# One layer of a hybrid streaming encoder: the low halves of every second piece of MLP weights come from an adding DMA

## The chip, the cores and the metric

The kernel runs on one core of a Trainium2 chip. The metric is the device time of one execution, in microseconds (us). Before the change the median of three runs is 1284.4 us (1284.13 to 1284.76).

## The reference

One layer with 256 tokens and 2048 model columns. A token mixer (a gated delta rule on eight heads, and an HGRN2 recurrence on eight heads) stands between two residual additions, and an MLP follows. The part that the change touches is the MLP:

```
def squared_relu_mlp(n, w1, w2):
    return jnp.square(jax.nn.relu(n @ w1)) @ w2

        n = rms_norm(h, norm_ffn_w[layer])
        h = h + squared_relu_mlp(n, w_ff1[layer], w_ff2[layer])
    return rms_norm(h, norm_final_w)
```

`w_ff1` is 2048 x 8192 and `w_ff2` is 8192 x 2048, both float32: 64 MB each, read once.

## The kernel before, in words

**Two halves of every weight.** TensorE multiplies in a rounded float32 format (fp32r). To keep float32 accuracy each operand is split in two: `hi` is the operand rounded to fp32r, and `lo` is what the rounding lost, `lo = w - hi`. A product is then made of three parts: hi times hi, hi times lo and lo times hi. For weights, `split` (L109 to L123) makes the two halves: ACT copies `w` into `hi` with the cast (L117), DVE subtracts `hi` from `w` into `lo` (L118).

**Stages.** Input projection and token mixer take up to about 460 us, the output projection up to 564 us, the first MLP product (FF1, `w_ff1`) from 564 to 927 us, the second (FF2, `w_ff2`) from 927 us to the end.

**Pieces.** The MLP weights come in 128 tiles `w` of 128 x 2048 (1 MB), 64 for each product, loaded by SP's DMA queue into a ring of three buffers. Each tile is split in two pieces of 128 x 1024. `hi` and `lo` of a piece live in two rings of three buffers each (`spool`). A piece of FF1 gives TensorE 8 matmuls with `hi` as the stationary operand (L700, 512 columns of `hT`, which holds the hi and lo of the activations side by side) and 8 with `lo` (L701, 256 columns), into four PSUM banks that belong to four blocks of FF columns; eight pieces make a group (`fg`), and groups take turns with two sets of four banks. A piece of FF2 gives 12 matmuls of 512 columns (L717): 8 with `hi`, 4 with `lo`, each with a block of the split activation `gs` as the stationary operand. The last three of FF2's 64 tiles are held and multiplied at the end (`held`); two of them, the tiles 61 and 62 counted from 0, are split into a buffer of their own (`keep`).

**What sets the order.** The kernel is written with a tile framework that puts the instructions of each engine in an order at build time. It goes by a timeline of its own, and it also gives each tile one of the buffers of its ring by that timeline. Waits between engines follow from reads and writes: whoever writes into a buffer again waits for the last reader of what it held. Each engine executes its own list in order. SP's list in the MLP is the loads of `w` alone; a load waits until the splits of the tile that held the buffer, three tiles earlier, are done. POOL has no work in the MLP until the last normalization.

Of the kernel before, what the change touches and what calls it, by code (L numbers as in the profile page):

```python
# [8 lines left out]
F32R = mybir.dt.float32r  # L9
AF = mybir.ActivationFunctionType  # L10
ALU = mybir.AluOpType
# [4 lines left out]
P = 128  # L16
# [57 lines left out]
def hybrid_block(ctx: ExitStack, tc: tile.TileContext, x, xt, w_in, w_ab, params, w_out, w_ff1, w_ff2,  # L74
                 norm_final_w, consts, out):
    nc = tc.nc
    PE, ACT, DVE, POOL, SP = nc.tensor, nc.scalar, nc.vector, nc.gpsimd, nc.sync
# [8 lines left out]
    spool = ctx.enter_context(tc.tile_pool(name="spool", bufs=3))  # L86
# [12 lines left out]
    def wtile():  # L99
        return wpool.tile([P, 2048], F32, tag="w", name="w")  # L100

    def acc_a():
        return psA.tile([P, 512], F32, tag="acc", name="acc")
# [7 lines left out]
    def split(w, n, hi=None, lo=None, pieces=1, eng=DVE):  # L111

        if hi is None:
            hi = spool.tile([P, n], F32R, tag="hi", name="hi")
            lo = spool.tile([P, n], F32R, tag="lo", name="lo")
        if pieces == 1:
            ACT.copy(hi, w)  # L117
            eng.tensor_tensor(out=lo, in0=w, in1=hi.bitcast(F32), op=ALU.subtract)  # L118
        else:
            for i in range(pieces):  # L120
                s = slice(i * n // pieces, (i + 1) * n // pieces)
                split(w[:, s], None, hi[:, s], lo[:, s], eng=eng)
        return hi, lo  # L123


# [85 lines left out]
    def gates():  # L211
        ab = spool.tile([P, KT, 2, 16], F32R, tag="hi", name="ab")
        split(wab, None, ab[:, :, 0, :], ab[:, :, 1, :])
        pab = mx("pab")
        for k in range(KT):
# [49 lines left out]
    def project(base, hd, chunk, dsts):  # L265
        accs = [acc_a() for _ in range(2)]
        for kh in range(2):
            first = base == 0 and hd == 0 and chunk == 0
            if first:
                w = w_first[kh]  # L270
            else:
                w = wtile()
                SP.dma_start(w, w_in[((base > 0) * NH + hd) * 4 + chunk * 2 + kh])
            for q in range(2):
                hi, lo = split(w[:, q * 1024:(q + 1) * 1024], 1024, pieces=2 if first else 1, eng=POOL if first else DVE)
                hi = hi.rearrange("p (k g c) -> p k g c", k=4, g=2)
                lo = lo.rearrange("p (k g c) -> p k g c", k=4, g=2)
                for kk in range(4):
                    k = kh * 8 + q * 4 + kk
                    for g in range(2):  # L280
                        PE.matmul(accs[g], lhsT=hi[:, kk, g, :], rhs=xT[:, k, :], start=(k == 0), stop=False)  # L281
                        PE.matmul(accs[g][:, T:], lhsT=lo[:, kk, g, :], rhs=xT[:, k, 0:T],  # L282
                                  start=False, stop=(k == KT - 1))
        if first:
            row_scales()
        for g in range(2):
            lot = mp.tile([P, T], F32, tag="lot", name="lot", bufs=2)
            ACT.copy(lot, accs[g][:, T:])
            DVE.tensor_tensor(out=lot, in0=accs[g][:, 0:T], in1=lot, op=ALU.add)
            (POOL if base == 0 else DVE).tensor_tensor(out=dsts[g], in0=lot, in1=rB, op=ALU.mult)  # L290
# [341 lines left out]
    def acc_b():  # L632
        return psB.tile([P, 512], F32, tag="accb", name="accb")
# [9 lines left out]
    for nh in range(2):  # L643
        accs = [acc_a() for _ in range(4)]
        for kp in range(8):
            w = wtile()
            SP.dma_start(w, w_out[nh * 8 + kp])
            for kk in range(2):
                k = 2 * kp + kk
                hi, lo = split(w[:, kk * 1024:(kk + 1) * 1024], 1024)  # L650
# [34 lines left out]
    def g(f):  # L685
        return gt[f // NG][:, f % NG, :]

    nfw = fp.tile([P, D], F32, tag="nfw", name="nfw")
    for fg in range(NF // 4):
        accs = [acc_a() if fg % 2 == 0 else acc_b() for _ in range(4)]  # L690
        for kq in range(4):
            w = wtile()
            SP.dma_start(w, w_ff1[fg * 4 + kq])
            for q in range(2):
                hi, lo = split(w[:, q * 1024:(q + 1) * 1024], 1024)
                for kk in range(2):
                    k = 4 * kq + 2 * q + kk
                    for f in range(4):
                        cs = slice(kk * 512 + f * P, kk * 512 + (f + 1) * P)
                        PE.matmul(accs[f], lhsT=hi[:, cs], rhs=hT[:, k, :], start=(k == 0), stop=False)  # L700
                        PE.matmul(accs[f][:, T:], lhsT=lo[:, cs], rhs=hT[:, k, 0:T], start=False, stop=(k == KT - 1))  # L701
        for f in range(4):
            lot = fp.tile([P, T], F32, tag="lotf", name="lotf", bufs=2)
            ACT.copy(lot, accs[f][:, T:])
            DVE.tensor_tensor(out=lot, in0=accs[f][:, 0:T], in1=lot, op=ALU.add)
            DVE.scalar_tensor_tensor(out=g(4 * fg + f), in0=lot, scalar=0.0, in1=lot, op0=ALU.max, op1=ALU.mult)
# [6 lines left out]
    def ff2(f, hf, c, gs, hl):  # L713
        hi, lo = hl[c // 2]
        cs = slice((c % 2) * 512, (c % 2 + 1) * 512)
        for a, ww in ((0, hi), (T, hi), (0, lo)):
            PE.matmul(accs[hf][c], lhsT=gs[:, a + hf * P:a + hf * P + P], rhs=ww[:, cs],  # L717
                      start=(f == 0 and a == 0 and ww is hi), stop=(f == NF - 1 and ww is lo))

    keep = None  # L720
    for f in range(NF):
        w = wtile()
        SP.dma_start(w, w_ff2[f])
        gs = fp.tile([P, 2 * T], F32R, tag="gs", name="gs", bufs=4)
        split(g(f), None, gs[:, 0:T], gs[:, T:])
        n = f - (NF - TAIL)
        if n == 0:
            keep = fp.tile([P, TAIL - 1, 2, D], F32R, tag="g0", name="keep")
        hl = []
        for q in range(2):  # L730
            qs = slice(q * 1024, (q + 1) * 1024)
            if 0 <= n < TAIL - 1:
                hl.append(split(w[:, qs], None, keep[:, n, 0, qs], keep[:, n, 1, qs]))
            else:
                hl.append(split(w[:, qs], 1024))
        if n >= 0:
            held.append((f, gs, hl))
            continue
        for q in range(2):
            for hf in range(2):  # L740
                for c in (2 * q, 2 * q + 1):
                    ff2(f, hf, c, gs, hl)
# [4 lines left out]
    for hf in range(2):  # L747
        pieces = [(c * 512, (c + 1) * 512) for c in range(3)]
# [74 lines left out]
```

## Time and profile before

| | |
|---|---|
| median of 3 runs | 1284.4 us (1284.13 to 1284.76) |
| the profiled execution, its own time | 1285.84 us |
| its span in the trace | 1283.9 us |
| mean granted TensorE clock in it | 0.992 |
| TensorE (PE) busy | 1252.5 us (98%) |
| DVE, ACT, POOL busy | 858.5 (67%), 673.8 (52%), 180.4 us (14%) |
| DMA | 229.65 MB, mean 179 GB/s |

How to read it: PE is matmuls, PEld the loading of their stationary operands, SPq and POOLq the instructions with which SP and POOL start DMAs. Each row of a group names the line of the kernel, the engine, the operation, what it writes and reads, and how often. "Idle before" is the time in which that engine had nothing to do just ahead of such an instruction, with the instruction that ended the wait. A DMA's "landing" is counted from its issue to the arrival of its last byte's signal.

### The profile page before, as it was taken

To read this page: it belongs to the slowest core of one execution; us is meant where nothing else is said; L and a number is where in the kernel's file an instruction comes from. 1 tells how busy PE (TensorE), PEld (TensorE's weight loads), DVE (VectorE), ACT (ScalarE), POOL (GpSimd) and SP (SyncE) were. 2 spreads that over 40 slices of the span, in tenths; PEclk is the share of its full clock that TensorE was granted. 3 is DMA by queue.
4 is the path that set the end of the run, shared out by engine and by line. 5 is a ranking of instruction groups with operands and counts; after the bars stand their busy time and mean duration, and the time that the engine had idled before them with its cause. 6 is when DMAs were issued, how large, how long until landed. Compare 5 with 4: busy or idle time off the path is not lost.

```text
span 1283.9 us, 18498 instructions
## 1 busy us (share of the span) xinstructions
PE 1252.5 (98%) x7290; PEld 1063.2 (83%) x7290; DVE 858.5 (67%) x1200; ACT 673.8 (52%) x972; POOL 180.4 (14%) x224
## 2 busy tenths in 40 slices
PE   6999999998899999999999999999999999999997
PEld 5888888877788887888888888888888888888885
DVE  8789999888867996565556555565555555555556
ACT  7567677655556874454444443444444444444453
POOL 4233433278301121000000000000000000000000
PEclk9999999998999999999999999999999999999999
DMA  7455555543423644455555555555555555555552
GB/s 289 166 160 184 174 180 192 171 140 131 149 100 131 217 151 168 154 203 191 194 173 190 196 174 189 197 175 186 197 195 190 188 191 192 194 194 197 197 200 95
DMA packets 34646, 229.65 MB, mean 179 GB/s; under 512 B 4408, under 2 KB 5184, under 8 KB 7808
## 3 DMA queue, kind: packets, MB, share of 16 engines
q1 hardware_dynamic: 32256, 225.32, 49.8%
q0 software_dynamic: 1728, 2.11, 1.3%
q8 instruction: 57, 0.93, 0.3%
q10 hardware_dynamic: 576, 1.05, 0.2%
q14 instruction: 29, 0.24, 0.1%
HBM read 225.83 MB, written 2.63 MB: 178 GB/s over the span
## 4 chain that ended last, share of the span: by engine, by line
PE 91%; DVE 3%; POOL 3%; issue 2%; DMA 1%; ACT 0%; SPq 0%; POOLq 0%; DVEq 0%; ACTq 0%
PE acc L281 15%; PE acc L717 14%; PE accb L717 13%; PE accb L700 9%; PE acc L700 9%; PE acc L282 8%; PE acc L655 7%; PE accb L701 5%; PE acc L701 5%; POOL Xt L419 1%; POOL X L421 1%; PE pd L575 1%; DVE xT L163 1%; DMA big<-in_xt_dram 1%; PE pk L363 1%
## 5 line engine op out<-in xcount | busy, mean ns | idle before, releaser
L118 DVE TENSOR_TENSOR lo<-w,hi 128x1024 fp32r<-128x1024 f32 x408 | 511.5, 1255 | 364.6 <-ACT hi L117 364.1
L117 ACT CAST hi<-w 128x1024 fp32r<-128x1024 f32 (+1 forms) x416 | 432.6, 1042 | 447.3 <-PE accb L717 177.2
L281 PE MATMUL acc<-xT,hi 128*128 128x512 f32 x1024 | 363.2, 401 | 9.6 <-ACT hi L117 8.5
L282 PE MATMUL acc<-xT,lo 128*128 128x256 f32 x1024 | 282.8, 285 | 4.8 <-DVE lo L118 4.7
L281 PEld LDWEIGHTS acc<-xT,hi 128*128 128x128 f32 x1024 | 191.0, 190 | 49.1 <-ACT hi L117 8.5
L282 PEld LDWEIGHTS acc<-xT,lo 128*128 128x128 f32 x1024 | 194.8, 191 | 12.1 <-DVE lo L118 6.2
L700 PE MATMUL acc<-hT,hi 128*128 128x512 f32 x512 | 181.3, 399 | 0.0
L700 PE MATMUL accb<-hT,hi 128*128 128x512 f32 x512 | 180.8, 398 | 0.0
L717 PE MATMUL accb<-hi,gs 128*128 128x512 f32 x496 | 170.6, 389 | 0.0
L701 PE MATMUL accb<-hT,lo 128*128 128x256 f32 x512 | 143.2, 281 | 0.0
L701 PE MATMUL acc<-hT,lo 128*128 128x256 f32 x512 | 142.8, 281 | 0.0
L717 PE MATMUL acc<-hi,gs 128*128 128x512 f32 x496 | 133.4, 389 | 0.0
L700 PEld LDWEIGHTS accb<-hT,hi 128*128 128x128 f32 x512 | 96.1, 188 | 23.9
L700 PEld LDWEIGHTS acc<-hT,hi 128*128 128x128 f32 x512 | 96.1, 188 | 23.4
L159 POOL TENSOR_TENSOR fin<-fin,cst 128x1 f32<-128x1 f32 x2 | 1.1, 566 | 777.0 <-PE accb L717 769.5
L717 PEld LDWEIGHTS acc<-hi,gs 128*128 128x128 f32 x496 | 93.0, 188 | 19.4
L717 PEld LDWEIGHTS accb<-hi,gs 128*128 128x128 f32 x496 | 93.1, 188 | 19.3
L701 PEld LDWEIGHTS acc<-hT,lo 128*128 128x128 f32 x512 | 96.5, 189 | 0.2
L701 PEld LDWEIGHTS accb<-hT,lo 128*128 128x128 f32 x512 | 96.6, 189 | 0.1
L717 PE MATMUL accb<-lo,gs 128*128 128x512 f32 x248 | 95.8, 389 | 0.0
L717 PE MATMUL acc<-lo,gs 128*128 128x512 f32 x248 | 77.2, 389 | 0.0
L717 PEld LDWEIGHTS acc<-lo,gs 128*128 128x128 f32 x248 | 46.6, 188 | 9.7
(248 smaller groups left out, 1323.6 us busy)
## 6 DMA issues: line engine op xcount, KB each, us to landing
w<-in_w_ff_dram SPq DMA_DIRECT2D x128, 1024.0 KB, 4.9
w<-in_w_in_dram SPq DMA_DIRECT2D x62, 1024.0 KB, 5.0
w<-in_w_out_dram SPq DMA_DIRECT2D x16, 1024.0 KB, 4.9
big<-in_xt_dram SPq DMA_DIRECT2D x4, 512.0 KB, 7.9
w<-in_w_in_dram SPq DMA_DIRECT2D x4, 512.0 KB, 8.1
h<-in_x_dram SPq DMA_DIRECT2D x2, 1024.0 KB, 9.2
dt<-scr_g POOLq DMA_DIRECT2D x8, 128.0 KB, 5.6
nfw<-in_norm_final_w_dram SPq DMA_DIRECT2D x1, 1024.0 KB, 4.7
```

The lines of the kernel that those rows point to most:

```text
L117: ACT.copy(hi, w)
L118: eng.tensor_tensor(out=lo, in0=w, in1=hi.bitcast(F32), op=ALU.subtract)
L163: DVE.scalar_tensor_tensor(out=dst[:, k, T:2 * T], in0=pt, scalar=wcol, in1=dst[:, k, 0:T].bitcast(F32), op0=ALU.mult, op1=ALU.subtract)
L281: PE.matmul(accs[g], lhsT=hi[:, kk, g, :], rhs=xT[:, k, :], start=(k == 0), stop=False)
L282: PE.matmul(accs[g][:, T:], lhsT=lo[:, kk, g, :], rhs=xT[:, k, 0:T], start=False, stop=(k == KT - 1))
L363: PE.matmul(pk0, lhsT=R[:, 1, 0:P], rhs=qk.rearrange("p a t -> p (a t)"), start=True, stop=True)
L419: POOL.tensor_tensor(out=t3, in0=X[:, j, j + 1:].unsqueeze(2).to_broadcast([np_, nr, ncol]), in1=X[:, j, 0:ncol].unsqueeze(1).to_broadcast ...
L421: POOL.tensor_tensor(out=X[:, j + 1:, 0:ncol], in0=X[:, j + 1:, 0:ncol], in1=t3, op=ALU.subtract)
L655: PE.matmul(accs[2 * hf + c], lhsT=st, rhs=ww[:, c * 512:(c + 1) * 512], start=(k == 0 and a == 0 and ww is hi), stop=(k == 2 * NH - 1 and ...
L700: PE.matmul(accs[f], lhsT=hi[:, cs], rhs=hT[:, k, :], start=(k == 0), stop=False)
L701: PE.matmul(accs[f][:, T:], lhsT=lo[:, cs], rhs=hT[:, k, 0:T], start=False, stop=(k == KT - 1))
L717: PE.matmul(accs[hf][c], lhsT=gs[:, a + hf * P:a + hf * P + P], rhs=ww[:, cs], start=(f == 0 and a == 0 and ww is hi), stop=(f == NF - 1 a ...
```

## The change

`split_ff` takes the place of `split` for the pieces of both MLP products (not for the two `keep` tiles). It counts pieces. An odd one (the first, third and so on, which is the first half of its tile `w`) is split as before. For an even one (the second half of its tile)

- ACT writes `-w`, cast to fp32r, into `lo` (`AF.Copy` with a scale of -1),
- POOL starts a DMA that reads the same 128 x 1024 weights from DRAM again and adds them onto `lo`, so that it holds `w - hi`,
- ACT copies `w` into `hi`.

DVE has no part in an even piece. There are 252 pieces that `split_ff` sees, so 126 such DMAs, 64 in FF1 and 62 in FF2, of 512 KB each.

```
+    pieces = [0]
+
+    def split_ff(w, src):
+
+        pieces[0] += 1
+        if pieces[0] % 2:
+            return split(w, 1024)
+        hi = spool.tile([P, 1024], F32R, tag="hi", name="hi")
+        lo = spool.tile([P, 1024], F32R, tag="lo", name="lo")
+        ACT.activation(lo, w, AF.Copy, scale=-1.0)
+        POOL.dma_start(lo, src, accum_op=ALU.add)
+        ACT.copy(hi, w)
         return hi, lo
...
             w = wtile()
             SP.dma_start(w, w_ff1[fg * 4 + kq])
             for q in range(2):
-                hi, lo = split(w[:, q * 1024:(q + 1) * 1024], 1024)
+                qs = slice(q * 1024, (q + 1) * 1024)
+                hi, lo = split_ff(w[:, qs], w_ff1[fg * 4 + kq, :, qs])
...
             if 0 <= n < TAIL - 1:
                 hl.append(split(w[:, qs], None, keep[:, n, 0, qs], keep[:, n, 1, qs]))
             else:
-                hl.append(split(w[:, qs], 1024))
+                hl.append(split_ff(w[:, qs], w_ff2[f, :, qs]))
```

In the changed kernel the lines of the diff stand 14 to 15 lines lower: L700 and L701 become L715 and L716, L717 becomes L732; the negated copy is L134, the DMA L135, the copy into `hi` L136. In what follows pieces are counted from 0 over both products, so the even pieces are those of DVE and the odd ones those of the DMA.

The build orders the engines anew. Three places are shown. In the rows the number behind a name is that of the tile, and a row ends with the semaphores that its instruction waits for: DMASW is a DMA issued by POOL, DMAHW one issued by SP.

**PE in FF1**, at the start of a second half of a tile `w`, before:

```order
L700 MATMUL accb_6595<-hT_4998,hi_6705 128x512 [waits Activation_49]
L701 MATMUL accb_6595<-hT_4998,lo_6706 128x256 [waits DVE_49]
L700 MATMUL accb_6596<-hT_4998,hi_6705 128x512
L701 MATMUL accb_6596<-hT_4998,lo_6706 128x256
L700 MATMUL accb_6597<-hT_4998,hi_6705 128x512
L701 MATMUL accb_6597<-hT_4998,lo_6706 128x256
```

and at the same piece now:

```order
L715 MATMUL accb_6615<-hT_4998,hi_6727 128x512 [waits Activation_49]
L715 MATMUL accb_6616<-hT_4998,hi_6727 128x512
L715 MATMUL accb_6617<-hT_4998,hi_6727 128x512
L715 MATMUL accb_6618<-hT_4998,hi_6727 128x512
L716 MATMUL accb_6615<-hT_4998,lo_6728 128x256 [waits DMASW5_49]
L716 MATMUL accb_6616<-hT_4998,lo_6728 128x256
```

Four matmuls with `hi` come first, then four with `lo`, of which the first waits for the DMA, then the rest in turns. This holds for two of the four odd pieces of a group of eight. The other two, and one even piece, are mixed. Counted from piece 26 on, PE takes in order: 26; 27 (hi x4, wait, rest); 28; 29 (hi x4, wait, rest); 30; 31 (hi x4 only); 32; 33 (hi x4 only); 31 (wait, the remaining 12); 33 (wait, the remaining 12); and then 34, which stands to its group as 26 does.

**ACT in FF1**, the casts of four consecutive pieces before:

```order
L117 CAST hi_6685<-w_6683 128x1024 [waits DMAHW2_49,PE_49,Activation_49]
L117 CAST hi_6705<-w_6683 128x1024 [waits DVE_49,PE_49]
L117 CAST hi_6727<-w_6725 128x1024 [waits DMAHW3_49,DVE_49,PE_49]
L117 CAST hi_6747<-w_6725 128x1024 [waits DVE_49,PE_49]
L117 CAST hi_6789<-w_6787 128x1024 [waits DMAHW4_49,DVE_49,PE_49]
```

and now:

```order
L117 CAST hi_6707<-w_6705 128x1024 [waits DMAHW2_49,PE_49,Activation_49]
L136 CAST hi_6727<-w_6705 128x1024 [waits PE_49,Activation_49]
L134 ACTIVATE lo_6728<-w_6705 128x1024 [waits DMASW1_49,PE_49]
L117 CAST hi_6750<-w_6748 128x1024 [waits DMAHW3_49,PE_49,Activation_49]
L136 CAST hi_6770<-w_6748 128x1024 [waits DVE_49,PE_49]
L134 ACTIVATE lo_6771<-w_6748 128x1024 [waits DMASW3_49,PE_49]
```

The negated copy stands behind the copy into `hi` of the same piece, although the source has it first. What it waits for on PE is the last matmul with the `lo` that its buffer held: for piece 29 that of piece 26, for 31 that of 28, for 33 that of 30, and for 35 (which stands to its group as 27 does) that of 31. The copy into `hi` ahead of it waits for the last matmul with `hi` of the same earlier piece, which is the instruction just before. The POOL DMA follows the negated copy at once; and the load of the tile `w` three tiles on, in SP's list, waits for the same negated copy, since that is the last reader of its buffer.

**PE in FF2**, most of a piece, before:

```order
L717 MATMUL acc<-hi,gs 128x512 [waits Activation_49]
L717 MATMUL acc<-hi,gs 128x512 x3
L717 MATMUL accb<-hi,gs 128x512
L717 MATMUL acc<-lo,gs 128x512 [waits DVE_49]
L717 MATMUL acc<-lo,gs 128x512
L717 MATMUL accb<-hi,gs 128x512
L717 MATMUL accb<-lo,gs 128x512
```

and now, with the parts of four pieces in turn:

```order
L732 MATMUL acc<-hi,gs 128x512 [waits Activation_49]
L732 MATMUL acc<-hi,gs 128x512 x3
L732 MATMUL accb<-hi,gs 128x512 x4
L732 MATMUL acc<-lo,gs 128x512 [waits DMASW4_49]
L732 MATMUL acc<-lo,gs 128x512
L732 MATMUL accb<-lo,gs 128x512 x2
L732 MATMUL acc<-hi,gs 128x512 x4
L732 MATMUL accb<-hi,gs 128x512 x4
L732 MATMUL acc<-lo,gs 128x512 [waits DVE_49]
L732 MATMUL acc<-lo,gs 128x512
L732 MATMUL accb<-lo,gs 128x512 x2
```

These 24 matmuls repeat through FF2: 8 with the `hi` of an even piece, 4 with the `lo` of an earlier odd piece (this is the wait for the DMA), 8 with the `hi` of the next odd piece, 4 with the `lo` of the even piece that the 24 began with. The odd pieces use two of the three `lo` buffers in turn and the even ones the third. So a negated copy waits for the last `lo` matmul of the odd piece before the last one, and the matmuls that need its DMA come 44 matmuls later. On ACT it stands behind the cast of an even piece that can be made 4 matmuls earlier.

More of the change, by code (lines that the diff above doesn't have):

```diff
@@ L122, in split @@
                 split(w[:, s], None, hi[:, s], lo[:, s], eng=eng)
+        return hi, lo
+    pieces = [0]
[8 more added lines that the diff above has]
+        ACT.copy(hi, w)
         return hi, lo
```

## The prediction

> **What bounds the kernel now.** I read the table of busy time by stage first, over the two MLP products (columns: length; busy time with instructions for PE, PEld, DVE, ACT, POOL; granted clock; DMA share; GB/s):
>
> ```profile
> 564.00:926.00 362.00, 362.00 (x2059) 314.09 (x2058) 204.22 (x268) 159.47 (x205) 0.00 (x0) 1.00 0.54 189
> 927.00:1250.00 323.00, 323.00 (x1426) 267.45 (x1425) 168.34 (x185) 145.65 (x182) 0.00 (x0) 1.00 0.55 194
> ```
>
> PE is busy in all of both stretches at a clock of 1.00. DVE and ACT are about half idle, POOL does nothing, the DMA engines are busy a little over half. The groups of the first stretch say what the splits cost and what they wait for:
>
> ```profile
> L118 DVE TENSOR_TENSOR lo<-w,hi 128x1024 fp32r<-128x1024 f32 x128 | 156.7, 1225 | 156.0 <-ACT hi L117 156.0
> L117 ACT CAST hi<-w 128x1024 fp32r<-128x1024 f32 x128 | 134.3, 1050 | 188.7 <-PE accb L700 95.0 <-PE acc L700 92.0 <-PE acc L655 1.7
> ```
>
> DVE waits for ACT, ACT waits for PE to give a buffer back: the splits run ahead of PE until the ring is full. So the DVE work that is taken away is off the path, and its removal alone is worth nothing here. What counts is whether the new way delivers `lo` in time.
>
> PE's own rate comes from its timeline. FF1, one piece:
>
> ```profile
> 649.74 0.40 PE L700 MATMUL accb<-hT,hi 128*128 128x512 f32 x1
> ...
> 652.23 0.40 PE L700 MATMUL accb<-hT,hi 128*128 128x512 f32 x1
> ...
> 652.46 0.28 PE L701 MATMUL accb<-hT,lo 128*128 128x256 f32 x1
> ...
> 652.57 0.40 PE L700 MATMUL accb<-hT,hi 128*128 128x512 f32 x1
> ...
> 652.66 1.05 ACT L117 CAST hi<-w 128x1024 fp32r<-128x1024 f32 x1 [1.78 <-PE accb L700]
> ```
>
> From 649.74 to 652.57 are eight pairs: 2.83 us a piece, 0.235 for a `hi` matmul and 0.118 for a `lo`. ACT starts its cast 0.20 us after PE's next matmul began (652.66 against 652.46): that is the price of handing a buffer back. FF2, three pieces of 12 matmuls:
>
> ```profile
> 1000.21 1.07 PE L717 MATMUL acc<-hi,gs 128*128 128x512 f32 x4
> ...
> 1002.93 1.07 PE L717 MATMUL acc<-hi,gs 128*128 128x512 f32 x4
> ...
> 1005.65 1.07 PE L717 MATMUL acc<-hi,gs 128*128 128x512 f32 x4
> ```
>
> 2.72 us a piece, 0.227 a matmul.
>
> **The change part by part.** *PE's new order* costs nothing by itself. Four `lo` matmuls in a row occur before in pairs:
>
> ```profile
> 15.29 0.63 PE L281 MATMUL acc<-xT,hi 128*128 128x512 f32 x2
> 15.76 0.40 PE L282 MATMUL acc<-xT,lo 128*128 128x256 f32 x2
> 15.99 0.40 PE L281 MATMUL acc<-xT,hi 128*128 128x512 f32 x1
> ```
>
> Two and two take 0.70 us, as two pairs in turns do.
>
> *ACT* gets 126 negated copies. Nearest rows: the cast above, 1.05 us, and an ACTIVATE of this size, 1.048:
>
> ```profile
> L172 ACT ACTIVATE junk<-big x4: 1039/1048/1063, 6.9 to 22.0; 128x1024 f32<-128x1024 f32 x4
> ```
>
> 126 x 1.05 = 132 us, on an engine that is idle for 202 of the first 362 us and 177 of the next 323: covered as work. As latency it counts, below. *DVE* loses 126 x 1.225 = 154 us that nobody waited for: 0.
>
> *Room.* How long may a negated copy, its DMA and the signal take, from the matmul that frees the `lo` buffer to the matmul that needs the new content? From PE's order in FF1 (a piece 2.83, four `hi` 0.94, the remaining twelve 1.88):
> - piece 27 (or 35: the remainder of 33, the whole of 34, four `hi`): 1.88 + 2.83 + 0.94 = 5.65
> - piece 29: two pieces and four `hi`: 6.60
> - piece 31: three pieces and twice four `hi`: 10.37
> - piece 33: four `hi`, a piece, four `hi`, a remainder: 6.59
> - FF2: 44 x 0.227 = 9.99
>
> *What has to fit in it.* In FF1 0.20 for the release, 1.05 for the copy into `hi` that stands ahead in ACT's list and is released only one matmul earlier, 1.05 for the negated copy, 0.10 for the two hand-overs to POOL and to PE (an estimate: half of the 0.20 just seen), and the DMA's landing D: 2.40 + D. In FF2 the cast ahead is already done: 1.35 + D.
>
> *D.* No DMA of before adds, and none of this size goes through POOL. The rows near it, first POOL's 256 KB load on an otherwise quiet stretch, in its timeline and in the DMA table of the window 253 to 262 us:
>
> ```profile
> 256.02 0.59 POOL L410 DMA_DIRECT2D X<-scr_a  x1
> ...
> 259.54 1.63 POOL L413 TENSOR_SCALAR_AFFINE_SELECT X<-X 64x1024 f32<-64x1024 f32 x1 [2.26 <-DMA X<-scr_a]
> ```
> ```profile
> q0 software_dynamic: 80, 0.26, 9.9%
> X<-scr_a POOLq DMA_DIRECT2D x1, 256.0 KB, 3.5
> ```
>
> It lands in 3.5 us, of which its packets take 9.9% of 9 us = 0.89: 2.6 us are fixed, the issue included. Then the weight loads, in the DMA table of FF1:
>
> ```profile
> q1 hardware_dynamic: 9354, 68.11, 53.5%
> w<-in_w_ff_dram SPq DMA_DIRECT2D x63, 1024.0 KB, 4.9
> ```
>
> 53.5% of 362 us for 68.11 MB is 2.84 us a MB, 2.98 us a tile. 512 KB take half, 1.49 us, and an addition onto `lo` has to fetch `lo` too: 2.98 if the second fetch costs as much, 1.49 if it is free. Last, company. The load of a tile `w` is released by the same negated copy, so each adding DMA starts together with 1 MB of weights. The 128 KB loads of `dt` show what that does:
>
> ```profile
> 65.03 0.61 POOL L351 DMA_DIRECT2D dt<-scr_g  x1 [3.77 <-DMA scr_g<-gr]
> ...
> 225.94 0.57 POOL L351 DMA_DIRECT2D dt<-scr_g  x1
> ```
> ```profile
> 66.95 0.33 SPq L273 DMA_DIRECT2D w<-in_w_in_dram  x1
> ...
> 226.43 6.31 SPq L273 DMA_DIRECT2D w<-in_w_in_dram  x2
> ```
> ```profile
> DMA to landing us min/median/max: 3.2/5.6/5.7
> ...
> dt<-scr_g POOLq DMA_DIRECT2D x1, 128.0 KB, 5.6
> ```
>
> (The first answer is over all eight, the second over the window 220 to 235 us.) The shortest takes 3.2 us; I take it for the first, which has the next load of weights 1.9 us behind it. The one at 225.94, with a load 0.5 us behind it, takes 5.6: +2.4 us. So D is between 2.6 + 1.49 = 4.1 (no company, free second fetch) and 2.6 + 2.98 + 2.98 = 8.6 (all of the tile ahead of it). With company it is 2.6 + 2.4 + 1.49 to 2.98 = 6.5 to 8.0. I take 7.5, near the upper end, because both operands are fetched by the same engines.
>
> The Trainium skill, "Collectives: The Full Stack", section "The bandwidth ceiling: the fold count and why AG ≠ RS ≠ AR", speaks against the change: an add in a DMA does not cost by the adding but by its two source reads, which share one ring, so that such a transfer runs at half rate. No run here shows it yet; by it D would be 8.0 and the loss in FF1 122 us, by a free second fetch (6.5) 74 us.
>
> *The sum.* With L = 2.40 + 7.5 = 9.9 in FF1, a wait is what L exceeds the room by, less the wait that lies inside the room already (each room contains the wait of the odd piece before it on PE). Piece 31: below 10.37, 0. Piece 33: 9.9 - 6.59 = 3.31. Piece 27 (35): 9.9 - 5.65 - 3.31 = 0.94. Piece 29: 9.9 - 6.60 - 0.94 = 2.36. Together 6.61 us a group, 16 groups: **106 us**. FF2: 1.35 + 7.5 = 8.85, under 9.99: 0, and if it were not covered, the excess over 9.99 is shared by two tiles, half of it for each of 61. The DMA engines have 2.98 + 2.98 = 5.96 us of work at most per tile against 5.44 us of PE in FF2, 4.47 at least: I count it as covered (if it isn't, 0.52 x 61 = 32 us). At the end the last adding DMA (the second half of tile 63) is needed some 45 matmuls, 10 us, after its buffer is free, and costs 0. The profiled execution has 1285.84 us beside a span of 1283.9; 1285.8 + 106 = 1392 in its terms, and as it stands 1.4 over the median, **1390 us** for the median.
>
> What is late next: a stalled PE frees `hi` late, but ACT's casts then still come with PE waiting on the DMA alone; the loads of `w` have three tiles of room.
>
> **The rivals.**
> - *Light DMA.* D from 3.3 to 5.6: no company to speak of. For it: SP's loads could get ahead or fall behind by the time ACT's order leaves. Against it: one negated copy releases both. At 4.3 L is 6.7; waits 0.11 + 0.94 + 0 a group, 17 us: 1301. At 5.6, 45 us: 1329.
> - *The DMA engines become the bound.* Speaking for it: the small POOL DMAs around 226 us. In the window 220 to 235 us:
>
> ```profile
> q0 software_dynamic: 176, 0.16, 11.9%
> ```
>
> 0.16 MB took 1.8 us of all 16 engines. At that price 512 KB are 5.9 us, with the tile 8.9 per 5.44 to 5.66 us of PE. Over 126 tiles that is +3.2 to +3.5 each, 420 us: 1705 as the far end. Those are short rows, mostly; halfway, at D = 10, FF1 loses 11.6 a group, 186 us, and FF2 (11.35 - 9.99) / 2 x 61 = 41: 1511.
> - *Not slower.* D of at most 3.2, the shortest `dt` row: L is 5.6, all four rooms hold, nothing is lost, and since no one waited for DVE nothing is won: 1284. It decides at D = 3.25. Against it: the plain 256 KB already took 3.5.
>
> The Trainium skill, "DMA: Bandwidth & Descriptors", section "Anatomy of one DMA — SWDGE (gpsimd) path", gives a POOL-issued DMA 2.0 us plus its bytes at 436 GB/s; for 512 KB that is 3.2 us, as an estimate, and would be this rival. The rows of `X` (3.5 for half the bytes) and `dt` (5.6) don't agree with it.
>
> **How the numbers follow.** The forecast (waits in FF1 alone, D from 5.6 to 8.8, 45 to 147 us) has 0.60, the light DMA 0.17, the DMA engines as the bound 0.18, not slower 0.05. The likeliest says 1390. Its own range is 1329 to 1432. To hold 8 in 10 it goes down to the light DMA at 4.3, 1301, and up to the heavy one at D = 10, 1511. A measurement of this kernel tells no change from 0.2%, 2.6 us. Slower by more: all but the last rival, and the edge of it, 0.95; within: 0.03; faster: 0.02, for what I don't see.
>
> **What would show it.** In the profile after: D by the landing of the adding DMA (7.5 us); PE waits on that DMA with some 6.6 us per group in FF1, at three of four odd pieces (about 3.3, 0.9, 2.4) and none in FF2; FF1 longer by 106 us, FF2 as before; DMA share of 0.7 to 0.9; ACT's negated copy at 1.05. It is wrong if D lies outside 5.6 to 8.8, if FF2 stalls too, if the loads of `w` come late, or if the negated copy isn't held up behind the copy into `hi`.

## The result and the profile after

| | before | changed |
|---|---|---|
| median | 1284.6 us (4 runs, 1284.13 to 1287.41) | 1535.3 us (4 runs, 1530.52 to 1542.23) |
| ratio, with 95% interval | | 1.195 (1.189 to 1.201) |
| span of the profiled execution | 1283.9 us | 1540.2 us |
| mean granted TensorE clock in it | 0.992 | 0.934 |

The forecast was 1390, in a range of 1301 to 1511. The sign was right; the loss is more than twice as large as forecast.

The busy time by stage of the changed kernel, FF1 and then FF2 (columns as in the prediction's first fence: length; busy time with instructions for PE, PEld, DVE, ACT, POOL; granted clock; DMA share; GB/s):

```profile
563.00:1111.00 548.00, 426.93 (x2070) 361.79 (x2069) 127.28 (x203) 220.31 (x269) 56.17 (x65) 0.87 0.76 187
1111.00:1525.00 414.00, 366.90 (x1514) 291.88 (x1513) 112.01 (x140) 213.81 (x258) 53.47 (x61) 0.96 0.92 233
```

The same two products before, in windows of nearly the same numbers of matmuls:

```profile
563.00:926.50 363.50, 363.50 (x2067) 315.26 (x2066) 205.72 (x270) 160.63 (x206) 0.00 (x0) 1.00 0.54 188
926.50:1270.00 343.50, 343.50 (x1518) 284.43 (x1517) 183.54 (x206) 154.36 (x198) 0.58 (x1) 1.00 0.53 187
```

They took 363.5 us in FF1 and 343.5 in FF2, at a clock of 1.00; now they take 548 and 414. PE is no longer busy all the time, and the time that it is busy has grown too, at a clock below 1.00. The page of the same execution gives PE's busy time, the groups that wait (busy time, mean ns of one, idle time before them with what ended it), and the DMAs (size, median us to landing):

```profile
PE 1338.6 (87%) x7290; PEld 1116.6 (72%) x7290; DVE 710.3 (46%) x1074; ACT 795.1 (52%) x1098; POOL 290.6 (19%) x350
...
L135 POOL DMA_DIRECT2D lo<-in_w_ff_dram x126 | 110.5, 877 | 908.5 <-ACT lo L134 401.5
...
L716 PE MATMUL accb<-hT,lo 128*128 128x256 f32 x512 | 140.4, 313 | 61.1 <-DMA lo<-in_w_ff_dram 61.1
L716 PE MATMUL acc<-hT,lo 128*128 128x256 f32 x512 | 140.6, 313 | 60.0 <-DMA lo<-in_w_ff_dram 60.0
...
L732 PE MATMUL acc<-lo,gs 128*128 128x512 f32 x248 | 82.7, 414 | 46.3 <-DMA lo<-in_w_ff_dram 46.3
...
w<-in_w_ff_dram SPq DMA_DIRECT2D x128, 1024.0 KB, 5.9
lo<-in_w_ff_dram POOLq DMA_DIRECT2D x126, 512.0 KB, 8.2
```

The landing of the adding DMA differs between the two products (DMA tables of the windows 700 to 900 us, in FF1, and 1111 to 1525 us, FF2):

```profile
lo<-in_w_ff_dram POOLq DMA_DIRECT2D x23, 512.0 KB, 8.1
...
lo<-in_w_ff_dram POOLq DMA_DIRECT2D x61, 512.0 KB, 9.6
```

The spans differ by 256.3 us. Three things add up to it: PE waits for the adding DMA in FF1, 61.1 + 60.0 = 121 us; it does so in FF2, 46 us; and the same 7290 matmuls keep it busy for 1338.6 - 1252.5 = 86 us longer. Together 253. FF1 has 33 of these waits. After the first group of eight pieces they come twice per group, at the pieces that stand as 29 and 33, and nearly all last 3.6 to 3.9 us.

One wait of FF1, in the timeline (start, duration, instruction; in brackets the idle time before and what ended it):

```profile
817.67 1.06 ACT L134 ACTIVATE lo<-w 128x1024 fp32r<-128x1024 f32 x1
...
819.02 0.88 POOL L135 DMA_DIRECT2D lo<-in_w_ff_dram  x1 [10.29 <-ACT lo L134]
...
822.11 0.28 PE L716 MATMUL accb<-hT,lo 128*128 128x256 f32 x1
822.30 1.05 ACT L136 CAST hi<-w 128x1024 fp32r<-128x1024 f32 x1 [1.74 <-PE accb L715]
823.26 1.05 ACT L134 ACTIVATE lo<-w 128x1024 fp32r<-128x1024 f32 x1
824.60 0.88 POOL L135 DMA_DIRECT2D lo<-in_w_ff_dram  x1 [4.71 <-ACT lo L134]
827.16 0.74 PE L716 MATMUL accb<-hT,lo 128*128 128x256 f32 x4 [3.85 <-DMA lo<-in_w_ff_dram]
```

The negated copy ends at 818.73, the DMA is issued at 819.02, and PE goes on at 827.16, 8.14 us later. At 822.30 the same chain begins for the next odd piece: 0.19 for the release, 0.96 until the copy into `hi` lets the negated copy start, 1.05 for that copy, 0.29 for the hand-over to POOL. With 8.14 the chain is 10.63 us long, where the forecast had 9.9.

What follows a wait is in the granted clock. Two waits and, in steps of 0.5 us, the step in which the clock falls to half and the one in which it comes back (columns: length, PE busy, clock, DMA share, GB/s):

```profile
707.15 1.22 PE L716 MATMUL acc<-hT,lo 128*128 128x256 f32 x4 [3.83 <-DMA lo<-in_w_ff_dram]
724.73 0.74 PE L716 MATMUL acc<-hT,lo 128*128 128x256 f32 x4 [3.79 <-DMA lo<-in_w_ff_dram]
```
```profile
705.00:705.50 0.50, 0.00 (x0) 0.91 1.15 229
...
712.00:712.50 0.50, 0.50 (x5) 0.77 1.15 229
```
```profile
725.50:726.00 0.50, 0.50 (x4) 0.89 1.22 262
...
729.00:729.50 0.50, 0.50 (x3) 0.70 1.06 238
```

In the steps between, the clock is 0.50 throughout. A mean of 0.91 in a step that ends at 0.50 means a fall at 705.41; in the same way it rises at 712.23, falls at 725.89 and rises at 729.30. The first fall came while PE was still waiting. So the clock was at half for 6.82 us around the first wait, with PE at work for the last 5.08 of them, and for 3.41 us behind the second. The four points lie 2, 4 and 1 times 3.41 us apart.

### The profile page after: what moved, and what is told of

It reads as the page before. It is cut to its first block, busy times and chain, and to the rows that moved or that the text cites. A ratio compares the mean times of both kernels' runs of the same rounds, so it can differ in the third digit from the quotient of the medians.

```text
span 1540.2 us, 18854 instructions
## 1 busy us (share of the span) xinstructions
PE 1338.6 (87%) x7290; PEld 1116.6 (72%) x7290; DVE 710.3 (46%) x1074; ACT 795.1 (52%) x1098; POOL 290.6 (19%) x350
## 3 DMA queue, kind: packets, MB, share of 16 engines
q10 hardware_dynamic: 576, 1.05, 0.2%
## 4 chain that ended last, share of the span: by engine, by line
PE 40%; issue 34%; DMA 15%; POOL 6%; DVE 3%; ACT 2%; POOLq 0%; DVEq 0%; ACTq 0%; SPq 0%
DMA lo<-in_w_ff_dram 14%; PE acc L295 13%; PE acc L296 7%; PE acc L669 6%; PE acc L732 5%; PE accb L732 5%; POOL lo L135 3%; ACT lo L134 1%; POOL Xt L433 1%; POOL X L435 1%; DMA w<-in_w_ff_dram 1%; PE pd L589 1%; DVE xT L177 0%; PE pk L377 0%; DVE E L560 0%
## 5 line engine op out<-in xcount | busy, mean ns | idle before, releaser
L118 DVE TENSOR_TENSOR lo<-w,hi 128x1024 fp32r<-128x1024 f32 x282 | 357.4, 1268 | 512.1 <-ACT hi L117 448.9
L117 ACT CAST hi<-w 128x1024 fp32r<-128x1024 f32 (+1 forms) x290 | 299.7, 1036 | 385.6 <-issue 159.0
L135 POOL DMA_DIRECT2D lo<-in_w_ff_dram x126 | 110.5, 877 | 908.5 <-ACT lo L134 401.5
L136 ACT CAST hi<-w 128x1024 fp32r<-128x1024 f32 x126 | 132.5, 1051 | 153.5 <-PE accb L715 57.6
L716 PE MATMUL accb<-hT,lo 128*128 128x256 f32 x512 | 140.4, 313 | 61.1 <-DMA lo<-in_w_ff_dram 61.1
L716 PE MATMUL acc<-hT,lo 128*128 128x256 f32 x512 | 140.6, 313 | 60.0 <-DMA lo<-in_w_ff_dram 60.0
L715 PE MATMUL accb<-hT,hi 128*128 128x512 f32 x512 | 192.7, 436 | 0.0
L715 PE MATMUL acc<-hT,hi 128*128 128x512 f32 x512 | 192.6, 435 | 0.0
L716 PEld LDWEIGHTS accb<-hT,lo 128*128 128x128 f32 x512 | 104.6, 219 | 69.1 <-DMA lo<-in_w_ff_dram 67.1
L134 ACT ACTIVATE lo<-w 128x1024 fp32r<-128x1024 f32 x126 | 132.7, 1053 | 42.5 <-PE accb L732 42.4
L716 PEld LDWEIGHTS acc<-hT,lo 128*128 128x128 f32 x512 | 104.6, 219 | 68.2 <-DMA lo<-in_w_ff_dram 66.3
L732 PE MATMUL acc<-hi,gs 128*128 128x512 f32 x496 | 139.6, 404 | 0.8 <-ACT gs L117 0.8
L732 PE MATMUL accb<-hi,gs 128*128 128x512 f32 x496 | 138.5, 401 | 0.0
L118 DVE TENSOR_TENSOR gs<-g,gs 128x256 fp32r<-128x256 f32 x64 | 27.1, 425 | 222.6 <-ACT gs L117 222.5
L715 PEld LDWEIGHTS accb<-hT,hi 128*128 128x128 f32 x512 | 107.5, 214 | 24.3
L715 PEld LDWEIGHTS acc<-hT,hi 128*128 128x128 f32 x512 | 107.1, 214 | 23.8
L732 PE MATMUL acc<-lo,gs 128*128 128x512 f32 x248 | 82.7, 414 | 46.3 <-DMA lo<-in_w_ff_dram 46.3
L732 PEld LDWEIGHTS acc<-hi,gs 128*128 128x128 f32 x496 | 96.7, 195 | 22.6 <-ACT gs L117 1.2
```

What stands on the lines that cost most here:

```text
L134: ACT.activation(lo, w, AF.Copy, scale=-1.0)
L135: POOL.dma_start(lo, src, accum_op=ALU.add)
```

## The experiments

"Changed" is the changed kernel at 1535.3 us; all ratios are to the kernel before, run beside each.

| run | edit to the changed kernel | time, us | ratio (95%) |
|---|---|---|---|
| e2 | matmuls with zeros fill FF1's waits | 1493.8 | 1.162 (1.154 to 1.171) |
| e4 | negation on DVE | 1514.0 | 1.178 (1.170 to 1.186) |
| e3 | the DMA copies and does not add | 1356.8 | 1.056 (1.052 to 1.059) |
| e7 | adding DMA in FF2 only | 1357.1 | 1.057 (1.048 to 1.065) |
| e5 | adding DMA for every fourth piece | 1434.5 | 1.117 (1.112 to 1.122) |
| e1 | own ring of four for these `lo` | 1416.5 | 1.102 (1.099 to 1.105) |
| e9 | fourth weight buffer | 1541.7 | 1.200 (1.198 to 1.203) |
| e8 | both rings | 1296.6 | 1.010 (1.005 to 1.015) |
| e6 | e1 and e3 together | 1327.0 | 1.033 (1.029 to 1.037) |
| e10 | e8, first three odd pieces by DVE | 1281.8 | 0.9974 (0.9964 to 0.9983) |
| e11 | kernel before, fourth weight buffer | 1285.1 | 1.0003 (0.9994 to 1.0013) |
| e12 | e10 with more DVE work | 1288.7 | 1.0028 (1.0017 to 1.0040) |

In the runs with a ring of their own for `lo` (e1, e6, e8, e10, e12) the last output tile `o` also shares the buffer of `g1`, to make room.

### Do the matmuls slow down because PE waits? (e2, e4)

```
+    zero = fp.tile([P, P], F32R, tag="zero", name="zero")
+    DVE.tensor_scalar(zero, ones, 0.0, None, ALU.mult)
...
                         PE.matmul(accs[f], lhsT=hi[:, cs], rhs=hT[:, k, :], start=(k == 0), stop=False)
+                        if q == 1 and kk == 0 and f < 4:
+                            for _ in range(2):
+                                PE.matmul(accs[f], lhsT=zero, rhs=hT[:, k, :], start=False, stop=False)
                         PE.matmul(accs[f][:, T:], lhsT=lo[:, cs], rhs=hT[:, k, 0:T], start=False, stop=(k == KT - 1))
```

> In the first product, eight matmuls with a weight tile of zeros, which add nothing to the sums, stand ahead of the matmuls that read the low part of each odd piece. PE gets about 16 x 4 x 8 x 0.227 = 116 us more work there, and is never idle for more than some 2 us. Theory A (the 65 us by which the first product's matmuls were busy longer come from the clock that falls after an idle time of 3.9 us): the granted clock there goes from 0.87 to 0.98 or more, the matmuls that read the low part go from 0.31 back to about 0.27 us, the added work fills time that was spent waiting, and the time is 1460 to 1490, less than the changed kernel's 1535 in spite of more work. Theory B (the matmuls were slow because the DMAs contend with them for the memory): clock and matmuls stay as slow, and the time is 1535 to 1650.

FF1 of this run, and one half of its `lo` matmuls:

```profile
562.00:1063.00 501.00, 488.05 (x2582) 409.77 (x2580) 127.05 (x205) 219.83 (x270) 56.09 (x65) 1.00 0.81 205
```
```profile
L721 PE MATMUL acc<-hT,lo 128*128 128x256 f32 x512 | 126.7, 285 | 6.5 <-DMA lo<-in_w_ff_dram 6.2
```

512 matmuls more, and 41 us less. The clock in FF1 is 1.00 where it was 0.87, a `lo` matmul takes 285 ns where it took 313, and the waits on the DMA fall from 60.0 to 6.2 us (in both halves together to 12), since PE now works through them. The time is 4 us above what theory A gave; theory B falls. The 63 us by which PE was busy longer in FF1 of the changed kernel (426.93 against 363.5) fit the half clock in size: a mean of 0.87 over 548 us means 142 us at half clock, the trace has PE at work in 125 of them, and half of that is 62 us. They lie behind 31 of the 33 waits, about 2 us each. In FF2, where no run fills the waits, the same working (32 us of work at half clock) gives 16 of the 23 us by which PE was busy longer; the other 7 stay open.

The second run makes the chain shorter instead:

```
-        ACT.activation(lo, w, AF.Copy, scale=-1.0)
+        DVE.tensor_scalar(lo, w, -1.0, None, ALU.mult)
```

> The negated copy of an odd piece is made by DVE and no longer by ACT, where it stood behind ACT's copy into the high part. Theory A (the chain of the forecast: release, high copy ahead, negated copy, DMA): the chain is shorter by the 1.05 us of the copy ahead, perhaps by 0.3 more if DVE's own instruction is faster, so each of the 33 waits of 3.86 us in the first product falls to about 2.6 us, 42 us less in all; if waits that short leave the granted clock up, another 30 to 65 us go, and the time is 1430 to 1495. Theory B (something other than this chain, such as the DMA engines or the loads, releases PE): 1530 to 1540. Theory C (DVE's work holds up the issue of the DMA on GpSimd): the issuing instruction gets longer than 0.88 us and the gain is lost, 1520 to 1560.

A wait, and the clock around it (first the timeline, then windows of 0.5 us); one of the two groups of such waits (the other, with `acc`, waits 45.5 us); the DMA:

```profile
717.91 1.22 PE L716 MATMUL acc<-hT,lo 128*128 128x256 f32 x4 [2.86 <-DMA lo<-in_w_ff_dram]
```
```profile
717.00:717.50 0.50, 0.00 (x0) 0.70 0.92 270
...
724.00:724.50 0.50, 0.50 (x5) 0.97 0.25 66
```
```profile
L716 PE MATMUL accb<-hT,lo 128*128 128x256 f32 x512 | 141.7, 317 | 47.2 <-DMA lo<-in_w_ff_dram 47.2
...
lo<-in_w_ff_dram POOLq DMA_DIRECT2D x126, 512.0 KB, 9.1
```

A wait is 1.0 us shorter (2.86 for 3.85), as the copy that stood ahead says. The waits of FF1 fall from 121 to 93 us; part of the gain goes back into the DMA, whose landing rises from 8.2 to 9.1. The total falls by 21 us, not by 42 or more, for the second part of theory A was wrong: waits of 2.8 us still halve the clock, from 717.2 to 724.0, and the matmuls stay at 315 to 317 ns. GpSimd's issue took 875 ns, so theory C falls.

### What does the adding cost? (e3)

```
-        POOL.dma_start(lo, src, accum_op=ALU.add)
+        POOL.dma_start(lo, src)
```

> The DMA of every odd piece copies the weights into the low part's tile and does not add them to what stands there, so this kernel multiplies by the whole weight where the changed one multiplies by the low part; all waits, copies and queues stay. Theory A (adding makes the DMA dear, since each element has to be fetched from two places): the landing falls from 8.2 us to 6.5 or less, the 16 engines' time for 512 KB from 2.67 us to 1.3 to 1.8, each wait of 3.86 us in the first product to about 2.2 or less, the waits of 46 us in the second product go nearly away, and the time is 1390 to 1450. Theory B (the cost is that of any DMA that GpSimd issues beside a 1 MB load): landing 8 us and a time of 1520 to 1540.

FF1 up to 985 us (its last 11 us or so lie in the next window), FF2 of this run, the issue on POOL, and the DMA:

```profile
562.00:985.00 423.00, 369.09 (x2023) 308.61 (x2022) 126.91 (x204) 215.96 (x264) 33.34 (x63) 0.99 0.66 237
985.00:1340.00 355.00, 354.08 (x1573) 293.25 (x1572) 114.96 (x144) 217.46 (x266) 33.24 (x63) 1.00 0.78 278
```
```profile
L135 POOL DMA_DIRECT2D lo<-in_w_ff_dram x126 | 66.6, 528 | 764.1 <-ACT lo L134 317.3
...
lo<-in_w_ff_dram POOLq DMA_DIRECT2D x126, 512.0 KB, 5.9
```

Theory A's causes hold, and its time, 1390 to 1450, was still too careful. Without the add the landing falls from 8.2 to 5.9 us, the issue from 0.877 to 0.528, FF2 has no waits, and FF1's waits fall from 121 to 28 + 27 us. They are of 0.6 to 1.7 us each but for one of 1.86 and one of 2.49, and behind all but these two the clock stays up. The engines' own time can be read from the share of the queue that POOL feeds, over 700 to 900 us, first the changed kernel and then this one:

```profile
q0 software_dynamic: 3419, 12.47, 33.3%
```
```profile
q0 software_dynamic: 4320, 15.73, 21.3%
```

33.3% of 200 us for 12.47 MB is 2.80 us for 512 KB; 21.3% for 15.73 MB is 1.42. With the add it is twice as much. The prediction had 2.98 and 1.49 for the two cases and a D of 8.0 by the Trainium skill's rule ("Collectives: The Full Stack", "The bandwidth ceiling: the fold count and why AG ≠ RS ≠ AR": two source reads, half rate). The trace agrees with that rule, 1.97 times the time.

### Are the two products' losses separate, and do they scale with the number of DMAs? (e7, e5)

```
-        if pieces[0] % 2:
+        if pieces[0] % 2 or pieces[0] <= 128:      (e7)
+        if pieces[0] % 4:                          (e5)
```

> The adding DMA is used in the second product alone (62 DMAs); the first product is split as before the change. Theory A (the losses of the two products are separate): the first product takes 363.5 us at clock 1.00, the second has waits of 40 to 55 us and 20 to 25 us of lower clock, time 1345 to 1360. Theory B (the second product's loss comes from starting late, out of the first): 1284 to 1320.

> Only every fourth piece has its low part made by the adding DMA (63 DMAs), the others are split by ACT and DVE. Theory A (two separate losses: latency, which is paid per DMA where the room is short, and throughput, which needs a DMA per 1 MB tile): in the second product the 16 engines need 2 x 3.44 + 2.67 = 9.6 us for two tiles where PE needs 10.9, so its 46 us of waits go; in the first product one of the two DMAs that are left per group of eight pieces has a short room, so one wait of 3.5 to 5 us per group stays, 16 in all, 56 to 80 us, with 25 to 45 us of lower clock behind them; time 1365 to 1410. Theory B (all of it is throughput of the DMA engines): no loss, 1284 to 1295. Theory C (loss in proportion to the number of DMAs): half of 251, 1410.

The stages, e7 and then e5:

```profile
564.00:926.50 362.50, 362.50 (x2061) 314.75 (x2060) 203.41 (x267) 160.75 (x207) 0.31 (x1) 1.00 0.53 189
926.50:1340.00 413.50, 366.58 (x1512) 291.13 (x1511) 109.85 (x137) 212.97 (x253) 53.97 (x62) 0.96 0.93 234
```
```profile
563.00:1054.00 491.00, 388.28 (x2051) 334.16 (x2050) 163.36 (x235) 187.78 (x236) 28.02 (x32) 0.89 0.60 172
1054.00:1410.00 356.00, 348.53 (x1508) 279.78 (x1507) 141.79 (x164) 184.11 (x222) 27.10 (x31) 1.00 0.78 227
```

In e7 FF2 loses what it lost in the changed kernel (413.5 and 414 us), so its 72 us are its own, and FF1 is left with the other 179: theory A of e7, within its 1345 to 1360. In e5 FF2's loss nearly goes (6 us of waits are left), and FF1 keeps one wait per group, but a longer one (16 of 5.7 to 6.7 us and one of 1.2, 104 us in all), with the clock at 0.89; the 1434.5 is 25 us beyond theory A's upper end, and why the wait is longer than the 3.5 to 5 us expected is not shown. Theory B of e5 is out. Its theory C named 1410 and is no nearer by its mechanism: half the DMAs cost 149 of 251 us, most of it in FF1. That FF2 is well with half the DMAs doesn't yet tell whether its bound was the DMA engines or the chain.

### Latency or throughput? (e1, e9, e8, e6)

```
-        lo = spool.tile([P, 1024], F32R, tag="lo", name="lo")
+        lo = fp.tile([P, 1024], F32R, tag="lo2", name="lo", bufs=4)
```

> The low parts of the odd pieces get a ring of four buffers of their own, so the negated copy and the adding DMA can start many pieces ahead of the matmuls that read the result; the work and the number of DMAs stay the same. Theory A (the loss is latency: the chain from a free buffer to the landed sum is longer than the room PE leaves it): the waits on the low part go in both products, TensorE's granted clock stays near 1.00, the first product takes about 363 us again instead of 548, and the time is about 1285 to 1300. Theory B (the loss is throughput: the 16 DMA engines need about 6.1 us per 1 MB piece with its share of the adding DMA, where PE needs 5.44): the waits get smaller but stay, mostly in the second product, the DMA share there stays above 0.9, and the time is 1330 to 1370. Theory C (the queue that issues the adding DMA, or ACT's copies, set the pace): near the changed kernel's 1535.

FF2 of this run's `hi` matmuls, and a piece of its timeline:

```profile
L732 PE MATMUL acc<-hi,gs 128*128 128x512 f32 x496 | 150.1, 404 | 49.5 <-ACT hi L117 47.6
...
w<-in_w_ff_dram SPq DMA_DIRECT2D x128, 1024.0 KB, 8.2
```
```profile
1209.07 1.06 ACT L134 ACTIVATE lo<-w 128x1024 fp32r<-128x1024 f32 x1 [6.17 <-DMA w<-in_w_ff_dram]
...
1210.03 1.03 ACT L117 CAST hi<-w 128x1024 fp32r<-128x1024 f32 x1
...
1211.11 1.19 PE L732 MATMUL acc<-hi,gs 128*128 128x512 f32 x4 [1.43 <-ACT hi L117]
```

The waits on the adding DMA are gone but for one of 6.6 us in FF1 and one of 1.6 at the end of FF2, and 119 us of the 251 with it. In its place ACT stands 6 us in a negated copy whose weights haven't landed, and the cast that PE wants next stands behind it. None of the three theories gave 1416: A's effect is there, and something new. The loads now take 8.2 us in place of 5.9, with three buffers for the weight tiles. If the 16 DMA engines were full (B), a fourth buffer would not help:

```
+            w = fp.tile([P, 2048], F32, tag="w2", name="w") if kq == 3 else wtile()
...
+        w = fp.tile([P, 2048], F32, tag="w2", name="w") if f % 4 == 3 else wtile()
```

(e9: this alone; e8: this, the ring for the odd pieces' `lo` with three buffers, and three in place of four for `gs`.)

> The changed kernel with a fourth 1 MB buffer for the weight tiles and nothing else; the low parts of odd pieces stay in the ring of three that all pieces share. Theory A (two buffers rule, one after the other: the low parts' ring sets the latency waits of the changed kernel, the weight tiles' ring only what is left once those are gone): the waits of 3.9 us in the first product stay, and the time is 1490 to 1540. Theory B (the weight tiles' ring is the cause of all of it): below 1350, as with both rings.

> The ring for the adding DMA's low parts (three buffers here) and a fourth buffer for the 1 MB weight tiles, where there were three; the scaled-activation tile has three buffers in place of four, for room. In the ring's run PE waited for ACT's high copies, which waited for weight loads that took 8.2 us to land, with the DMA engines busy 0.84 to 0.88. Theory A (the loads were late because each waited for one of three buffers): the loads start earlier, the waits fall by half or more, the DMA share goes to 0.95, time 1310 to 1380. Theory B (the 16 engines are the bound at 0.88 already): 1405 to 1420.

FF1 and FF2 of e8; its DMAs over 600 to 900 us; and the one wait that is left in FF1:

```profile
562.00:932.00 370.00, 358.93 (x2060) 315.73 (x2059) 127.04 (x202) 222.38 (x270) 57.85 (x66) 0.98 0.99 280
932.00:1275.00 343.00, 341.34 (x1503) 281.18 (x1503) 104.41 (x137) 209.67 (x254) 52.47 (x60) 1.00 0.98 277
```
```profile
q0 software_dynamic: 7798, 28.41, 52.9%
q1 hardware_dynamic: 7785, 56.68, 47.1%
...
w<-in_w_ff_dram SPq DMA_DIRECT2D x54, 1024.0 KB, 8.2
lo<-in_w_ff_dram POOLq DMA_DIRECT2D x54, 512.0 KB, 8.3
```
```profile
L716 PE MATMUL acc<-hT,lo 128*128 128x256 f32 x512 | 144.2, 283 | 8.8 <-DMA lo<-in_w_ff_dram 8.8
```

This settles it. The DMAs are as slow as in the changed kernel (8.3 us to landing, the loads slower than there), there are as many of them, the engines show busy 0.99, and yet PE is busy nearly all the time: 1296.6 us, better than theory A's 1310 to 1380. So throughput was not the bound, in FF2 as little as in FF1, and a share of 0.92 of the DMA engines did not mean a limit. Everything was latency, in two rings one behind the other. The fourth weight buffer alone does nothing (e9: 61.5 + 59.2 us of waits in FF1, 48.4 in FF2, 1541.7 us), as its theory A said, for the first ring still rules.

> The ring of four buffers of the first experiment and the copying DMA of the third (the DMA does not add, so the product is with the whole weight). Theory A (latency and the engines' time for the add are the whole loss): the engines need 3.44 + 1.4 = 4.9 us for a tile where PE needs 5.44 to 5.7, no wait is left, clock 0.99, time 1284 to 1292. Theory B (something else stays, such as ACT's 126 further copies, GpSimd's issue, or contention of the weight loads with a second stream): 1300 or more, with the waits on ACT's high copies as in the ring's run.

The ring with the lighter copying DMA and three weight buffers gives 1327, so theory B. PE waits for the `hi` casts behind weight loads that land in 6.9 us here, 4.9 before the change; in FF2 that is 18.8 us of waits. By what e8 shows this is the second ring; the copying DMA with a fourth weight buffer was not run.

### A version that is as fast as the kernel before, and a little faster (e10, e11, e12)

```
-        if pieces[0] % 2:
+        if pieces[0] % 2 or pieces[0] <= 6:        (e10, on top of e8)
```

> Both rings as in the run of 1297 us, and the first three odd pieces of the first product split by DVE, not by the adding DMA: in that run PE waited 8.8 us for the first low part, and ran at a lower clock behind it, in all 37.8 us for a group of four pieces' sums that takes 24.7 in the kernel before. Theory A: these 13 us go, and the time is 1280 to 1287, equal to the kernel before within 0.3%, for PE is then busy without a gap in both. Theory B (the wait moves to the first piece that the DMA makes): 1292 to 1300.

> The kernel before the change with a fourth buffer for the weight tiles: no adding DMA. In the run with both rings a pair of matmuls of the first product started every 0.347 us, in the kernel before every 0.353. Theory A (this comes from the change of the split, such as DVE's lighter load): no difference, 1283 to 1286. Theory B (it comes from the place of the buffers): the pair takes 0.347 us, and the time is 1276 to 1280.

> The kernel of 1281.8 us, in which DVE subtracts again for every odd piece that the DMA makes: three subtractions of 256 columns each into a tile that nobody reads, so DVE has three quarters of the work back that the change took from it, and what the result needs is unchanged. There a pair of matmuls in the first product started every 0.347 us, in the kernel before every 0.353, which is 6 us over the product. Theory A (the pair is faster because DVE reads and writes less beside it): the pair goes back to 0.351 or more and the time to 1285 to 1288. Theory B (DVE's load has no part in it): 0.347 us, and 1280 to 1283.

e12 adds this to e10:

```
         ACT.copy(hi, w)
+        for i in range(3):
+            scr = fp.tile([P, 256], F32R, tag="scr", name="scr")
+            s = slice(i * 256, i * 256 + 256)
+            DVE.tensor_tensor(out=scr, in0=w[:, s], in1=hi[:, s].bitcast(F32), op=ALU.subtract)
```

The same 160 us of FF1 in the kernel before, in e10 and in e12 (columns as above; the number behind PE's time is that of its matmuls):

```profile
640.00:800.00 160.00, 160.00 (x908) 138.67 (x907) 88.81 (x113) 68.05 (x85) 0.00 (x0) 1.00 0.54 188
```
```profile
640.00:800.00 160.00, 160.00 (x925) 139.91 (x924) 55.42 (x85) 96.58 (x116) 25.05 (x29) 1.00 1.01 284
```
```profile
640.00:800.00 160.00, 160.00 (x908) 138.95 (x907) 90.42 (x169) 95.51 (x114) 25.13 (x29) 1.00 1.00 277
```

e10 has no wait in FF1 and takes 1281.8 us, 0.26% less than the kernel before (interval 0.17 to 0.36%): theory A. The gain is in FF1, where PE gets through 925 matmuls in the time of 908, a pair in 0.346 us in place of 0.352; FF2 gives some of it back in 3 us of waits. A fourth buffer without the DMA changes nothing (e11, theory A; 907 matmuls in that window). With DVE's work put back (e12) the pair is at 0.352 again, and the time at 1288.7, just over theory A's upper end.

So the pair's time goes with DVE's load in these four. It doesn't go with DVE's work at the same moment, though: worked out pair by pair from the timeline of 640 to 860 us, a pair of the kernel before takes 0.353 us with DVE busy beside it and 0.353 with DVE idle, and one of e10 0.347 either way. And in e1, where DVE did as little, it was about 0.353. How DVE's load, or something that goes with it, sets the pair's time stays open.

## Why the prediction was right and wrong

- **What bounds the kernel before; ACT's 126 copies covered; PE's new order free**: right. In e10 ACT has those copies, PE stands in another order, and nothing is lost.
- **DVE's work worth 0**: right for the changed kernel. With all waits gone FF1 is about 6 us shorter where DVE does less (e10) and not where it does more again (e12); that DVE's load is the cause is not shown, for e1 doesn't follow it.
- **The chain and the rooms in FF1**: right. L was 10.63 where 9.9 was taken, 0.6 of it from the landing, 0.2 from POOL's hand-over. At L = 10.63 the prediction's own rule gives 4.04 for piece 33, 0.94 for 27, 3.09 for 29 and nothing for 31, 8.07 us a group, 129 in all; 121 were measured, 106 forecast. The pattern was another: two waits of some 3.8 per group, none at 27. The half clock behind the wait of 33 stretches the next room by 1.7 to 2.5 us, more than the 0.94 that 27 would wait; this is argued from the sizes. e3 agrees with it: there the clock stays up, and three waits come in each group, as the rule has them (1.60, 0.68 and 0.95 us from 706.86 us on).
- **D = 7.5**: mis-sized, 8.1 in FF1 and 9.6 in FF2. The Trainium skill's rule of two source reads, with 8.0 and 122 us, was nearer than the choice made; it stood in the prediction as a sentence, without changing the sum. The Trainium skill's other rule ("DMA: Bandwidth & Descriptors", section "Anatomy of one DMA — SWDGE (gpsimd) path", 3.2 us by its figures, an estimate) disagrees with every run: the shortest landing of an adding DMA was 5.4 us (e1), that of a copying one 3.8 (e3, e6).
- **The sum, "a wait is what L exceeds the room by"**: this is the step that failed. It took PE's rate after a wait as that before. The waits of some 3.8 us halved the clock for 3.4 or 6.8 us, and so beside 167 us of waits PE was busy 86 us longer, 78 of them by the half clock as worked out above. e2 shows the cause for FF1, with the clock back at 1.00 by filling the waits.
- **FF2, "1.35 + 7.5 = 8.85, under 9.99: 0"**: wrong by the same D, taken for both products though in FF2 the loads and the adds run together nearly always (DMA share 0.92). With 9.6 the chain is 10.95, and the prediction's formula gives 0.96 / 2 x 61 = 29 us; 46 were measured, and the rest stays open. That the DMA engines could carry it ("I count it as covered") was right: e8 does the same work in FF2 with PE waiting 1.7 us.
- In terms of the forecast: 1390, + 15 for FF1's waits, + 46 for FF2's, + 86 for PE's longer busy time = 1537, for 1535 measured.
- **The rivals**: the heavy DMA's 1511 was the nearest number, by the wrong mechanism. The engines were never the bound; a small ring was. The light DMA and "not slower" fall with D = 8.2.
- **"Loads of `w` have three tiles of room"**: right for the changed kernel (e9), wrong as soon as the first ring was widened (e1).

## What to carry to other kernels

When work moves from an engine to a DMA, its time per piece matters less than how many pieces ahead it can start: the same DMAs cost 251 us with three shared buffers, 11 with a ring of their own and a fourth weight buffer, and nothing once the first three odd pieces were made by DVE. Price a stall of TensorE at its length plus the half clock behind it, here about another 2 us for each wait of some 3.8. And when one ring is widened, look for the next one in line before calling the DMA engines full: a busy share of 0.92 went with PE waiting, 0.99 with PE at work.

## What the runs showed of the hardware that wasn't expected

- **The clock can fall after gaps well under 3.4 us.** It stayed at half for 3.41 and 6.82 us, which agrees with the Trainium skill, "TensorE: Matmul & The Clock Gate", section "Part 1: The HAM clock gate" (a free-running window of 3413 ns, half rate after an idle window). The same page of the Trainium skill, section "HAM oscillation — how this bites in real kernels", has the rule to leave no gap above about 3.4 us. Here gaps of 2.86 us (e4), and of 2.49 and 1.86 (e3), were enough; those of e3 up to 1.7 us left the clock at 1.00. The 3.41 us that ended at 717.2 in e4 had PE busy for some 1.2 of them, so they needn't be idle throughout. Nor does the length of a gap decide alone: in FF2 of the changed kernel gaps of 2.87 and 3.12 us (ended at 1178.11 and 1379.35) left the clock at 1.00, and one of 2.20 (ended at 1398.18) did not. That it depends on where a gap falls among the steps of 3.41 us is a guess that no run tests. Two rows of e3, the longest wait and the clock around it:

```profile
576.62 0.74 PE L716 MATMUL acc<-hT,lo 128*128 128x256 f32 x4 [2.49 <-DMA lo<-in_w_ff_dram]
```
```profile
576.00:584.00 8.00, 7.38 (x33) 0.79 0.57 199
```

- **An adding DMA costs its issuer too**: 0.877 us on POOL for 512 KB, 0.528 for the plain copy of the same tile.
- **A landing time is elastic**: 512 KB added took 8.1 us beside FF1's loads and 9.6 beside FF2's, and the 1 MB loads went from 4.9 to 8.2 us, while the work got done in time where the rings allowed it.
